# Decoding the sink group by two sequences at a time in a streaming-encoder step

## The chip, the cores and the metric

The kernel runs on one core of a Trainium2 chip. The metric is device time in microseconds (us) for one whole step, median over several executions. TensorE (PE) does the matmuls, VectorE (DVE), ScalarE (ACT) and GpSimd (POOL) the rest, and SyncE's queue (SP) issues nearly all transfers between HBM and SBUF. Each engine takes its instructions strictly in the order in which they were laid down for it, and semaphores make an engine wait for another's result.

## The reference

One layer of a hybrid encoder, on 512 prompt tokens and 8 decode sequences of 16 new tokens each (640 columns in all). One input projection is split between two groups of attention heads, whose outputs are normalised, joined and projected; a SwiGLU block and a final RMSNorm follow.

```python
def sample_layer(x, ck_a, cv_a, ck_b, cv_b, ...):          # 8 sequences of 16 new tokens
    qa, ka, va, qb, kb, vb = split_proj(rmsnorm(x, norm_mix) @ w_in)
    qb, kb = rope_partial(qb, pos), rope_partial(kb, pos)
    ...
    # group B: 16 query heads on 2 key/value heads, 128 cached keys + 16 new ones, learned sinks
    ob = band_attend(qb.reshape(b, 1, s, N_KV_B, GQA_R, HEAD_DIM),
                     concat([ck_b, kb], axis=1)[:, None], concat([cv_b, vb], axis=1)[:, None],
                     ones((1, keep_b + s)), sink=sinks.reshape(N_KV_B, GQA_R))
    return merge_and_ffn(x, oa, ob, ...), ka, va, kb, vb

def band_attend(q, k, v, valid, bias=None, sink=None):
    s = einsum('bgqhrd,bgkhd->bghrqk', q, k) * HEAD_DIM ** -0.5
    m = maximum(max(s, -1), sink);  p = exp(s - m)
    w = p / (sum(p, -1) + exp(sink - m))
    return einsum('bghrqk,bgkhd->bgqhrd', w, v)
```

For group B a decode sequence is therefore small: for each of the two key/value heads, 128 rows (8 query heads by 16 tokens) against 144 keys.

## The kernel before

Nearly all of the time is dense matmul work on PE: a weight tile is split into a high and a low part (`split`, L226 on ACT, L227 on DVE), and each product is three fp32r matmuls (`mm3`, L235 to L237) of 128x128 weights on 320 columns. I call these the **main** matmuls. The input projection does its first columns in plain form (`dense`, `proj`); the rest of it, and later the whole SwiGLU block, goes through `quartet`, a Strassen-like scheme with seven products on combined operands. Those combined operands of the input are made by `combine(k0, k1)` (L866 on DVE, L867 and L869 on POOL, then splits), for input tiles 0 to 2, 3 to 5 and 6 to 7.

Everything else, the attention above all, is written as Python generators that are drawn in between the main matmuls. `tick()` is called after each group of six main matmuls and, at a given `rate`, calls `pump()`; a pump runs one generator up to its next `yield`. I call that a **visit**. The streams (`heads`, `decode`, `combine`, later `norm`) take turns. A generator that yields `"part"` says that its next visit uses only a part of the PE array (64 rows or 64 columns), and the pump tries to run two such visits in a row. `get` hands out SBUF slots from fixed lists (S slots and twelve W slots) and itself pumps when a list is empty. A scheduler then settles the order of each engine.

`decode_b` is the decode attention of group B. It handles the 8 sequences one by one, in two halves of four. For one sequence it needs four visits: the scores (L596, two matmuls of 64 rows, one for each key/value head, each in a PSUM bank of its own) with the softmax on DVE and ACT (L601 to L611); two visits that only let time pass; four transposes of the weights (L341, through `tr`) and their copy out of PSUM on ACT (L621); the values (L626, on 64 columns) with the copy into the output tile `o_s` (L629). With the loads this makes 37 visits. `o_s` lies in a W slot; at the end it is stored to `ob_d` (L632), the slot goes back to the list, and `combine(6, 8)` is put into its queue:

```python
        dma(out=ob_d[:, :, SP:].rearrange("t p c -> p t c"), in_=o_s)
        n.put("W", os_b)
        n.put("S", kb, vb)
        n.add("combine", combine(6, 8))
```

The visits of `decode_b` are drawn in beside the last prompt heads of group B (`prompt_b`: scores L425, transposes L341 in `flip`, values L464) and beside four plain projections that end the first part of the input projection. After these, `n.drain()` runs what is left, and the quartets begin. About 240 us later comes the stage of the output projection of group B (`w_out_b`), into which the `heads` of group A (`prompt_a`), its decode (`decode_a`: L662, L671 to L678, L713) and the norm of group B (`norm_b`) are drawn in the same manner.

Of the kernel before, what the change touches and what calls it, by code (L numbers as in the profile page):

```python
# [7 lines left out]
AF = mybir.ActivationFunctionType  # L8
# [5 lines left out]
P = 128  # L14
# [4 lines left out]
SP = 512  # L19
# [3 lines left out]
DS = 16  # L23
CA = 256
CB = 128
# [294 lines left out]
def build(nc, tc, io, pools):  # L320
    n = Net(nc, tc, io, pools)
    dma = nc.sync.dma_start
# [12 lines left out]
    sinks, sink_d = col(16), col(2)  # L335
# [19 lines left out]
    qkv_d, sb_d = dram("qkv_d", (3, 8, P, TOK)), dram("sb_d", (P, 8, P))  # L355
# [13 lines left out]
    for kt in range(KT):  # L369
# [10 lines left out]
        own, hl = pair("S")  # L380
# [194 lines left out]
    def decode_b():  # L575
        os_b = n.get("W")
        o_s = sh(os_b, 8, P)
        for hf in range(2):
            ko, vo, qo, qraw = (n.get("S") for _ in range(4))
            k, v, q = sh(ko, 4, CB + DS), sh(vo, 4, P), sh(qo, 4, P)  # L580
            dma(out=k[:, :, :CB], in_=io["ckb"][:, 4 * hf:4 * hf + 4])
            dma(out=v, in_=io["cvb"][:, 4 * hf:4 * hf + 4])
            dma(out=sh(qraw, 8, 64), in_=sb_d[:, :, 64 * hf:64 * hf + 64])
# [3 lines left out]
            nc.gpsimd.tensor_copy(sh(qo, 4, 8, DS), sh(qraw, 8, 64).rearrange("p t (b s) -> p b t s", b=4))  # L587
            n.put("S", qraw)
            yield "part"
            for bb in range(4):  # L590
                b = 4 * hf + bb
                pss, pts = [], []
                for j in range(2):
                    rows = slice(64 * j, 64 * j + 64)
                    ps = n.bank()[:, :CB + DS]
                    nc.tensor.matmul(ps, q[rows, bb], k[rows, bb], start=True, stop=True)  # L596
                    pss.append(ps)
                for j, ps in enumerate(pss):
                    mx, den, se = n.small(1), n.small(1), n.small(1)
                    sk = sink_d[:, j:j + 1]  # L600
                    nc.vector.tensor_reduce(mx, ps, AX, ALU.max)  # L601
# [5 lines left out]
                    nc.scalar.activation(se, mx, AF.Exp, bias=sk)  # L607
                    nc.vector.tensor_tensor(den, den, se, ALU.add)
                    nc.vector.reciprocal(den, den)
                    nc.vector.tensor_scalar(pt[:, :CB], ex[:, :CB], den, None, ALU.mult)  # L610
                    nc.vector.tensor_scalar(pt[:, CB + DS * b:CB + DS * b + DS], ex[:, CB:], den, None, ALU.mult)  # L611
                    pts.append((t, pt))
                yield
                yield
# [6 lines left out]
                nc.scalar.activation(pt2[:, :4 * P], ps, AF.Identity)  # L621
                yield "part"
                po = n.bank()[:, :P]
                for x, vv in enumerate((v[:, bb], vb[:, SP:])):
                    for j in range(2):
                        nc.tensor.matmul(po[64 * j:64 * j + 64], vv[:, 64 * j:64 * j + 64],  # L626
                                         pt2[:, P * (2 * x + j):P * (2 * x + j) + P], start=x == 0, stop=x == 1)
# [4 lines left out]
        dma(out=ob_d[:, :, SP:].rearrange("t p c -> p t c"), in_=o_s)  # L632
        n.put("W", os_b)
        n.put("S", kb, vb)
        n.add("combine", combine(6, 8))
# [212 lines left out]
        n.put("S", x)  # L848

    sums = [[None] * 7 for _ in range(8)]  # L850
    thirds = []

    def combine(k0, k1):

# [2 lines left out]
        for kt in range(k0, k1):  # L857
# [9 lines left out]
            tt(s2, s1, a11, ALU.subtract)  # L867
            s3 = third[:, HT * (kt % 3):HT * (kt % 3) + HT]
            tt(s3, a21, a11, ALU.subtract)  # L869
            thirds.append((third, s3))  # L870
# [265 lines left out]
    parts = []  # L1136
# [293 lines left out]
```

## Time and profile before

| what | value |
|---|---|
| runs | 2541.51, 2544.72, 2547.5 us; median 2544.72 us |
| profiled execution | 2540.53 us, with a span of 2538.8 us from first to last instruction |
| PE busy | 2488.2 us, 98% of the span |
| DVE, ACT, POOL busy | 1966.8 us (77%), 1057.6 us (42%), 703.2 us (28%) |
| scores of group B's decode (L596) | from 210.7 to 268.1 us of the span |
| mean granted TensorE clock | 0.995 |

The numbers of the profile come from that one profiled execution, which took 4.2 us less than the median of the three runs. A line of the profile such as `L596` is a line of the kernel; `out<-in` names the tiles; `[0.66 <-DVE S L611]` behind a row says that the engine sat idle for 0.66 us until DVE's line 611 was done with an S tile.

### The profile page before, as it was taken

Reading aid. Unit: us, or ns where it says so; the run is one execution under the profiler, and the core shown is the slowest. Engines: PE = TensorE matmul, PEld = TensorE weight load, DVE = VectorE, ACT = ScalarE, POOL = GpSimd, SP = SyncE. Lnnn points to the kernel's source line nnn. Section 1 sums busy time; section 2 is a strip of 40 time slices with the busy share of each in tenths; the row PEclk is TensorE's granted clock in tenths of the full one; section 3 lists DMA queues with packets and bytes.
Section 4 is the critical chain, followed back from the end, with each engine's and each line's share of the span. In section 5 each row is a group of like instructions: output and inputs, shape, how many; then the busy total and the mean of one; then the engine's idle time right before and its main releaser. Section 6 shows DMA issues by size and latency. Waiting matters only on the chain.

```text
span 2538.8 us, 44665 instructions
## 1 busy us (share of the span) xinstructions
PE 2488.2 (98%) x17325; PEld 2422.5 (95%) x17325; DVE 1966.8 (77%) x2930; ACT 1057.6 (42%) x1701; POOL 703.2 (28%) x566
## 2 busy tenths in 40 slices
PE   8999999989999999999999999999999999999997
PEld 8898899988899999999999999999999999999997
DVE  6666767685567787788888888888889877777797
ACT  5445333355555544344343334334334333333343
POOL 0001211110021133323332332323335433333453
PEclk9999999999999999999999999999999999999998
DMA  6234433467863434444344334334437765666655
GB/s 197 83 98 131 148 123 127 135 235 244 263 219 139 140 130 138 149 156 134 128 130 146 120 127 144 133 128 131 145 120 247 249 170 165 182 171 172 186 160 183
DMA packets 191604, 401.68 MB, mean 158 GB/s; under 512 B 22496, under 2 KB 83936, under 8 KB 191392
## 3 DMA queue, kind: packets, MB, share of 16 engines
q1 hardware_dynamic: 167056, 344.75, 41.5%
q0 software_dynamic: 23184, 52.77, 7.6%
q8 instruction: 136, 2.23, 0.4%
q10 hardware_dynamic: 1152, 1.31, 0.2%
q14 instruction: 76, 0.62, 0.1%
HBM read 311.14 MB, written 86.87 MB: 157 GB/s over the span
## 4 chain that ended last, share of the span: by engine, by line
PE 87%; DVE 7%; DMA 2%; issue 1%; ACT 1%; POOL 0%; SPq 0%; DVEq 0%; ACTq 0%; POOLq 0%
PE dn L235 18%; PE dn L237 17%; PE dn L236 17%; PE at L235 10%; PE at L236 10%; PE at L237 10%; DVE W L227 2%; PE at L341 2%; PE at L464 1%; DMA W<-w_in 1%; PE at L425 1%; DVE S L793 1%; DMA W<-xT 1%; PE at L713 0%; ACT W L226 0%
## 5 line engine op out<-in xcount | busy, mean ns | idle before, releaser
L226 ACT ACTIVATE W<-W 128x1024 fp32r<-128x1024 f32 (+2 forms) x662 | 640.0, 968 | 1050.5 <-PE dn L236 554.9
L235 PE MATMUL dn<-S,W 128*128 128x320 f32 x3374 | 1055.9, 313 | 10.3 <-ACT W L226 5.1
L237 PE MATMUL dn<-S,W 128*128 128x320 f32 x3374 | 1046.3, 310 | 7.9 <-DVE W L227 7.7
L236 PE MATMUL dn<-S,W 128*128 128x320 f32 x3374 | 1044.7, 310 | 0.3 <-DVE S L227 0.3
L227 DVE TENSOR_TENSOR W<-W,W 128x1024 fp32r<-128x1024 f32 (+2 forms) x662 | 798.0, 1206 | 89.7 <-ACT W L226 85.5
L235 PEld LDWEIGHTS dn<-S,W 128*128 128x128 f32 x3374 | 635.0, 188 | 27.1 <-issue 13.8
L237 PEld LDWEIGHTS dn<-S,W 128*128 128x128 f32 x3374 | 634.4, 188 | 13.4 <-DVE W L227 11.7
L236 PEld LDWEIGHTS dn<-S,W 128*128 128x128 f32 x3374 | 635.1, 188 | 1.1 <-DVE S L227 0.6
L237 PE MATMUL at<-S,W 128*128 128x320 f32 x1834 | 567.4, 309 | 1.2 <-DVE W L227 1.0
L235 PE MATMUL at<-S,W 128*128 128x320 f32 x1834 | 567.6, 309 | 0.9 <-ACT W L226 0.9
L236 PE MATMUL at<-S,W 128*128 128x320 f32 x1834 | 567.0, 309 | 0.0
L774 POOL TENSOR_TENSOR W<-W,W 128x1024 f32<-128x1024 f32 (+2 forms) x84 | 181.3, 2158 | 771.9 <-DVE W L227 617.7
L237 PEld LDWEIGHTS at<-S,W 128*128 128x128 f32 x1834 | 344.5, 188 | 2.2 <-DVE W L227 1.9
L235 PEld LDWEIGHTS at<-S,W 128*128 128x128 f32 x1834 | 344.7, 188 | 1.4 <-ACT W L226 1.4
L236 PEld LDWEIGHTS at<-S,W 128*128 128x128 f32 x1834 | 344.7, 188 | 0.0
L793 DVE TENSOR_TENSOR S<-S,dn 128x320 f32<-128x320 f32 x398 | 182.2, 480 | 76.2 <-PE dn L237 75.7
L783 POOL TENSOR_TENSOR W<-W,W 128x1024 f32<-128x1024 f32 (+2 forms) x84 | 186.5, 2220 | 182.7 <-DVE W L227 136.4
L793 DVE TENSOR_TENSOR S<-S,at 128x320 f32<-128x320 f32 x292 | 138.3, 482 | 96.4 <-PE at L237 94.8
L767 DVE TENSOR_TENSOR W<-W,W 128x1024 f32<-128x1024 f32 (+2 forms) x86 | 119.9, 1394 | 37.7 <-DMA W<-w_gate 26.1
L771 DVE TENSOR_TENSOR W<-W,W 128x1024 f32<-128x1024 f32 (+2 forms) x86 | 97.9, 1139 | 59.1 <-DMA W<-w_up 29.4
L1082 POOL DMA_DIRECT2D S<-act_d x161 | 88.0, 547 | 166.7 <-PE dn L237 80.1
L1146 DVE TENSOR_TENSOR S<-S,half 128x320 fp32r<-128x320 f32 x147 | 119.8, 835 | 1.9
(157 smaller groups left out, 1703.2 us busy)
## 6 DMA issues: line engine op xcount, KB each, us to landing
S<-act_d POOLq DMA_DIRECT2D x161, 320.0 KB, 3.9
W<-w_gate SPq DMA_DIRECT2D x88, 512.0 KB
W<-w_up SPq DMA_DIRECT2D x88, 512.0 KB
W<-w_in SPq DMA_DIRECT2D x66, 512.0 KB
W<-w_down SPq DMA_DIRECT2D x64, 384.0 KB
act_d<-half SPq DMA_DIRECT2D x147, 160.0 KB
act_d<-S SPq DMA_DIRECT2D x147, 160.0 KB
W<-w_down SPq DMA_DIRECT2D x68, 320.0 KB
```

The costliest lines, as they stand in the source:

```text
L226: self.nc.scalar.activation(hi, src, AF.Identity)
L227: self.nc.vector.tensor_tensor(lo, src, f(hi), ALU.subtract)
L235: mm(out, a[0], b[0], start=first, stop=False)
L236: mm(out, a[0], b[1], start=False, stop=False)
L237: mm(out, a[1], b[0], start=False, stop=last)
L767: nc.vector.tensor_tensor(b12[:, w], b12[:, w], b22[:, w], sub)
L771: nc.vector.tensor_tensor(s6[:, w], b11[:, w], b12[:, w], sub)
L774: eng.tensor_tensor(b11[:, w], b22[:, w], s6[:, w], sub)
L783: eng.tensor_tensor(b21[:, w], b21[:, w], s6[:, w], sub)
L793: add = lambda o, a, b: nc.vector.tensor_tensor(o, a, b, ALU.add)
L1082: nc.gpsimd.dma_start(out=r(sh(t, 2, HT)), in_=r(act_d[which, :, j]))
L1146: nc.vector.tensor_tensor(r(src), src, hi, ALU.subtract)
```

## The change

`decode_b` handles two sequences in one step, so four steps instead of eight. The scores of both sequences go side by side into the same two banks (columns 0 and 256), eight transposes into two banks come in one visit, the values of both go into one bank, and the scores of the next step are issued in the same visit as the values. Four visits lie between the scores and the transposes instead of two, and two more between transposes and values; both halves are loaded near the start. With the loads this makes 31 visits, and 5 marks `"part"` instead of 16. Since `combine(6, 8)` can now be queued at another point than before, `thirds` becomes a table by tile number instead of a list.

```diff
+        def score(step):
+            (_, k, _, q), two = parts[step // 2], (2 * step % 4, 2 * step % 4 + 1)
+            pss = [n.bank() for _ in range(2)]
+            for i, bb in enumerate(two):
+                for j, ps in enumerate(pss):
+                    rows = slice(64 * j, 64 * j + 64)
+                    nc.tensor.matmul(ps[:, 256 * i:256 * i + CB + DS], q[rows, bb], k[rows, bb],
+                                     start=True, stop=True)
+            out = []
+            for i in range(2):
+                b, pts = 2 * step + i, []
                 for j in range(2):
-                    rows = slice(64 * j, 64 * j + 64)
-                    ps = n.bank()[:, :CB + DS]
-                    nc.tensor.matmul(ps, q[rows, bb], k[rows, bb], start=True, stop=True)
-                    pss.append(ps)
-                for j, ps in enumerate(pss):
+                    ps, sk = pss[j][:, 256 * i:256 * i + CB + DS], sink_d[:, j:j + 1]
                     mx, den, se = n.small(1), n.small(1), n.small(1)
-                    sk = sink_d[:, j:j + 1]
                     nc.vector.tensor_reduce(mx, ps, AX, ALU.max)
                     ...
+        parts = [load(0)]
+        yield
+        turn(parts[0][0], parts[0][3])
+        yield "part"
+        weights = score(0)
+        for step in range(4):
+            if step == 0:
+                parts.append(load(1))
+            for _ in range(4):
                 yield
-                yield
+            if step == 0:
+                turn(parts[1][0], parts[1][3])
+            turned = []
+            for pts in weights:
                 ps = n.bank()
                 for i, (_, pt) in enumerate(pts):
                     for x in range(2):
                         tr(ps[:, P * (2 * x + i):P * (2 * x + i) + P], pt[:, P * x:P * x + P])
                 n.put("S", *(t for t, _ in pts))
-                pt2 = n.get("S")
-                nc.scalar.activation(pt2[:, :4 * P], ps, AF.Identity)
-                yield "part"
-                po = n.bank()[:, :P]
-                for x, vv in enumerate((v[:, bb], vb[:, SP:])):
+                turned.append(n.get("S"))
+                nc.scalar.activation(turned[-1][:, :4 * P], ps, AF.Identity)
+            yield
+            yield
+            yield "part"
+            own, _, v, _ = parts[step // 2]
+            po = n.bank()
+            for i, pt2 in enumerate(turned):
+                for x, vv in enumerate((v[:, (2 * step + i) % 4], vb[:, SP:])):
                     for j in range(2):
-                        nc.tensor.matmul(po[64 * j:64 * j + 64], vv[:, 64 * j:64 * j + 64],
+                        nc.tensor.matmul(po[64 * j:64 * j + 64, P * i:P * i + P], vv[:, 64 * j:64 * j + 64],
                                          pt2[:, P * (2 * x + j):P * (2 * x + j) + P], start=x == 0, stop=x == 1)
-                n.put("S", pt2)
-                nc.vector.tensor_copy(o_s[:, :, DS * b:DS * b + DS], po.rearrange("p (t s) -> p t s", t=8))
-                yield "part" if bb < 3 else None
-            n.put("S", ko, vo, qo)
+            n.put("S", *turned)
+            if step < 3:
+                weights = score(step + 1)
+            for i in range(2):
+                at = DS * (2 * step + i)
+                nc.vector.tensor_copy(o_s[:, :, at:at + DS],
+                                      po[:, P * i:P * i + P].rearrange("p (t s) -> p t s", t=8))
+            if step % 2:
+                n.put("S", *own)
```

Lines after the change are numbered up to 30 higher: scores L599, softmax L607 to L617, copy of the transposes L642, values L651, copy to `o_s` L658, the store L662; `combine`'s loads of the input are L889 and L890 (L859 and L860 before), a quartet's loads L783 (L753).

**PE, a step of the decode.** Before, a values visit and the next score visit of one sequence (`dn` is the running projection, `at` a small bank):

```order
L235 MATMUL dn_2680<-S_61_197,W_489_2830 128x320
L626 MATMUL at_2854<-S_492_2846,S_462_2705 64x128 x2
L626 MATMUL at_2854<-S_492_2846,S_5_83 64x128 x2
L596 MATMUL at_2866<-S_461_2704,S_463_2706 128x144
L596 MATMUL at_2868<-S_461_2704,S_463_2706 128x144
L236 MATMUL dn_2680<-S_62_198,W_489_2830 128x320
```

After, the first step, from its second four transposes to the scores of the second step:

```order
L341 MATMUL at_2377<-cst,S_369_2237 128x128 x2
L341 MATMUL at_2377<-cst,S_373_2250 128x128 x2
L235 MATMUL dn_2439<-S_25_125,W_412_2441 128x320
L236 MATMUL dn_2439<-S_26_126,W_412_2441 128x320
L651 MATMUL at_2464<-S_399_2375,S_346_2138 64x128 x2
L651 MATMUL at_2464<-S_399_2375,S_5_83 64x128 x2
L651 MATMUL at_2464<-S_401_2382,S_346_2138 64x128 x2
L651 MATMUL at_2464<-S_401_2382,S_5_83 64x128 x2
L599 MATMUL at_2473<-S_345_2137,S_347_2139 128x144
L599 MATMUL at_2474<-S_345_2137,S_347_2139 128x144
L599 MATMUL at_2473<-S_345_2137,S_347_2139 128x144
L599 MATMUL at_2474<-S_345_2137,S_347_2139 128x144
```

Twice as much stands in one place, half as often; two main matmuls stand between the transposes and the values that read their copies.

**SP, the end of the decode.** Before: loads of the first quartets, then the store of `o_s` (W_344), then the load of the last operand of `combine` (tile 7), which has been given the W slot of `o_s`, then more loads of the quartets:

```order
L753 DMA W_582_3430<-w_in 128x1024
L753 DMA W_557_3186<-w_in 128x1024
L753 DMA W_583_3432<-w_in 128x1024
L632 DMA ob_d<-W_344_2136 128x8x128
L846 DMA o_va<-S_552_3176 128x640
L847 DMA qkv_d<-S_552_3176 128x640
L860 DMA W_545_3099<-xT 128x640
L753 DMA W_568_3298<-w_in 128x1024
```

After:

```order
L783 DMA W_543_3170<-w_in 128x1024
L889 DMA W_527_3021<-xT 128x640
L662 DMA ob_d<-W_344_2136 128x8x128
L783 DMA W_545_3174<-w_in 128x1024
L890 DMA W_528_3022<-xT 128x640
L876 DMA o_va<-S_532_3051 128x640
L877 DMA qkv_d<-S_532_3051 128x640
L783 DMA W_544_3172<-w_in 128x1024
```

The store and the last load of `combine` now stand ahead of most of the first quartet's weights. On PE the last values visit moved from row 1588, just ahead of the quartets (row 1601), to row 1473, 130 rows ahead of them (row 1603).

**ACT, the start of the `w_out_b` stage.** The visits there are drawn from the same turn-taking counter and the same slots, so that their order changes too, up to PE row 4215. Before, the first split for the third product of this stage (W_954) stands behind a block of table loads (`ACT_TABLE_LOAD`, 21 rows ahead), exponentials and copies:

```order
L573 ACTIVATE S_921_5849<-at_5850 128x512
L573 ACTIVATE S_923_5862<-at_5863 128x512
L673 ACTIVATE S_930_5890,sm_5887<-S_929_5889,sm_5886 128x256
L674 ACTIVATE S_930_5890,sm_5888<-S_929_5889,sm_5886 128x16
L454 ACTIVATE S_946_5946<-at_5941 128x512
L454 ACTIVATE S_948_5959<-at_5954 128x512
L226 ACTIVATE W_955_5975<-W_954_5974 128x1024
```

After, it stands ahead of the table loads (W_942):

```order
L438 ACTIVATE S_837_5512,sm_5698<-S_837_5512,sm_5697 128x512
L573 ACTIVATE W_856_5578<-at_5722 128x512
L226 ACTIVATE W_943_5963<-W_942_5962 128x1024
L276 ACT_TABLE_LOAD
L276 ACTIVATE sm_5756<-sm_5754 128x6
L438 ACT_TABLE_LOAD
L438 ACTIVATE S_831_5506,sm_5764<-S_831_5506,sm_5763 128x128
```

The split moved by 24 rows on ACT, while the matmuls that read it moved by 4 rows on PE (3412 before, 3408 after).

More of the change, by code (lines that the diff above doesn't have):

```diff
@@ L577, in decode_b, with load @@
         o_s = sh(os_b, 8, P)
-        for hf in range(2):
-            ko, vo, qo, qraw = (n.get("S") for _ in range(4))
-            k, v, q = sh(ko, 4, CB + DS), sh(vo, 4, P), sh(qo, 4, P)
+        def load(hf):
+            own = [n.get("S") for _ in range(4)]
+            k, v, q = sh(own[0], 4, CB + DS), sh(own[1], 4, P), sh(own[2], 4, P)
             dma(out=k[:, :, :CB], in_=io["ckb"][:, 4 * hf:4 * hf + 4])
             dma(out=v, in_=io["cvb"][:, 4 * hf:4 * hf + 4])
-            dma(out=sh(qraw, 8, 64), in_=sb_d[:, :, 64 * hf:64 * hf + 64])
+            dma(out=sh(own[3], 8, 64), in_=sb_d[:, :, 64 * hf:64 * hf + 64])
@@ L584, in decode_b @@
             nc.gpsimd.tensor_copy(k[:, :, CB:],
                                   kb[:, SP + 64 * hf:SP + 64 * hf + 64].rearrange("p (b s) -> p b s", b=4))
-            yield
-            nc.gpsimd.tensor_copy(sh(qo, 4, 8, DS), sh(qraw, 8, 64).rearrange("p t (b s) -> p b t s", b=4))
-            n.put("S", qraw)
-            yield "part"
-            for bb in range(4):
-                b = 4 * hf + bb
-                pss, pts = [], []
-                for j in range(2):
-                    rows = slice(64 * j, 64 * j + 64)
-                    ps = n.bank()[:, :CB + DS]
-                    nc.tensor.matmul(ps, q[rows, bb], k[rows, bb], start=True, stop=True)
-                    pss.append(ps)
-                for j, ps in enumerate(pss):
+            return own, k, v, q
@@ new lines, in turn @@
+        def turn(own, q):
+            nc.gpsimd.tensor_copy(sh(own[2], 4, 8, DS), sh(own[3], 8, 64).rearrange("p t (b s) -> p b t s", b=4))
+            n.put("S", own.pop())
+        def score(step):
[9 more added lines that the diff above has]
+                b, pts = 2 * step + i, []
+                for j in range(2):
+                    ps, sk = pss[j][:, 256 * i:256 * i + CB + DS], sink_d[:, j:j + 1]
@@ L612, in decode_b @@
                     pts.append((t, pt))
+                out.append(pts)
+            return out
+        parts = [load(0)]
[7 more added lines that the diff above has]
+            for _ in range(4):
                 yield
-                yield
+            if step == 0:
+                turn(parts[1][0], parts[1][3])
+            turned = []
+            for pts in weights:
                 ps = n.bank()
@@ L869, in combine @@
             tt(s3, a21, a11, ALU.subtract)
-            thirds.append((third, s3))
+            thirds[kt] = third, s3
             for which, x in ((3, s1), (1, s2), (6, a12)):
```

3 lines of the change are left out of this document (1 added, 2 removed).

## The prediction

> **What bounds the kernel now.** I read the page first: PE's share and the chain that ended last.
>
> ```profile
> PE 2488.2 (98%) x17325; PEld 2422.5 (95%) x17325; DVE 1966.8 (77%) x2930; ACT 1057.6 (42%) x1701; POOL 703.2 (28%) x566
> PE 87%; DVE 7%; DMA 2%; issue 1%; ACT 1%; POOL 0%; SPq 0%; DVEq 0%; ACTq 0%; POOLq 0%
> ```
>
> PE is the bound, so that a change off PE counts only where PE waits. How much there is to win is read by stage: columns are PE busy, its weight loads, DVE, ACT, POOL, then granted clock, DMA share, GB/s.
>
> ```profile
> 205.00:280.00 75.00, 71.89 (x506) 62.26 (x505) 51.46 (x175) 40.16 (x112) 15.22 (x23) 1.00 0.42 135
> 280.00:320.00 40.00, 36.62 (x241) 35.01 (x240) 28.36 (x30) 12.55 (x15) 7.53 (x4) 1.00 0.44 150
> 320.00:500.00 180.00, 178.40 (x1210) 177.17 (x1210) 122.22 (x129) 55.81 (x58) 35.75 (x15) 1.00 0.37 129
> 500.00:560.00 60.00, 56.87 (x371) 53.03 (x370) 48.04 (x101) 30.52 (x50) 11.45 (x14) 0.97 0.74 246
> 560.00:580.00 20.00, 16.12 (x135) 14.13 (x138) 9.86 (x26) 14.64 (x38) 1.48 (x5) 0.91 0.48 165
> 580.00:760.00 180.00, 178.94 (x1594) 150.97 (x1583) 112.26 (x336) 95.02 (x244) 21.95 (x41) 1.00 0.73 243
> ```
>
> The undisturbed quartets (third row) lose 1.6 us in 180, and one main matmul takes 180/1210 = 0.149 us there. PE is idle for 3.1 us beside the decode (75 - 71.89) and 3.4 us in the first quartets behind it; the `w_out_b` stage, which the change reorders too, loses 3.1, 3.9 and 1.1 us in its three stretches, and in the middle one the clock is down. The waits of the first two stretches (total, times, longest):
>
> ```profile
> PE at L341 <- DVE S L610: 1.8, 4, 1.0
> PE at L341 <- DVE S L611: 1.3, 4, 0.7
> PE dn L237 <- DVE W L227: 1.2, 2, 1.0
> PE dn L235 <- ACT W L226: 1.1, 1, 1.1
> PE dn L235 <- ACT S L226: 0.6, 1, 0.6
> PE at L235 <- ACT W L226: 0.4, 1, 0.4
> ```
>
> 3.1 us are transposes that wait for the decode's softmax; the rest are splits that the quartets wait for.
>
> **A. Fewer visits on PE.** A visit costs more than its matmuls, because PE changes between full and partial use of the array. A values visit, a score visit, and both in a row:
>
> ```profile
> 242.93 0.31 PE L237 MATMUL dn<-S,W 128*128 128x320 f32 x1
> 243.17 0.66 PE L626 MATMUL at<-S,S 128*64 128x128 f32 x8
> 244.01 0.31 PE L236 MATMUL dn<-S,W 128*128 128x320 f32 x1
> ...
> 236.62 0.31 PE L237 MATMUL dn<-S,W 128*128 128x320 f32 x1
> 236.86 0.52 PE L596 MATMUL at<-S,S 64*128 64x144 f32 x4
> 237.56 0.31 PE L236 MATMUL dn<-S,W 128*128 128x320 f32 x1
> ...
> 253.78 0.31 PE L235 MATMUL dn<-S,W 128*128 128x320 f32 x1
> 254.05 0.66 PE L626 MATMUL at<-S,S 128*64 128x128 f32 x8
> 254.64 0.52 PE L596 MATMUL at<-S,S 64*128 64x144 f32 x4
> 255.09 0.42 PE L236 MATMUL dn<-S,W 128*128 128x320 f32 x1
> 255.34 0.31 PE L237 MATMUL dn<-S,W 128*128 128x320 f32 x1
> ```
>
> In each piece I take the time from the main matmul before the visit to the second one after it, less two main steps (0.30): 1.08 - 0.30 = 0.78 us for values, 0.94 - 0.30 = 0.64 for scores, 1.56 - 0.30 = 1.26 for both in a row. Before, there are eight of each, and in the order four pairs stand in a row: 8 x 0.78 + 8 x 0.64 - 4 x 0.16 = 10.7 us. After, there are four of each with twice the matmuls, three pairs in a row. The added matmuls cost at most 0.59 (254.64 - 254.05) for values and 0.45 (255.09 - 254.64) for scores, which gives 3 x 2.30 + 1.37 + 1.09 = 9.4 us. If they step by their columns as the main ones do (0.149 x 128/320 = 0.06 and 0.149 x 144/320 = 0.067), they cost 0.48 and 0.27, and the sum is 8.2. So A is -1.3 to -2.5 us; I take -1.8, since in the third step the order tears the values in two, which gives back about one change of use (0.3).
>
> **B. The transposes' waits.** They do not simply go: four softmax chains instead of two run through DVE one behind the other. From a score visit on:
>
> ```profile
> 228.97 0.52 PE L596 MATMUL at<-S,S 64*128 64x144 f32 x4
> 229.62 0.30 DVE L601 TENSOR_REDUCE sm<-at 128x1 f32<-128x144 f32 x1
> 231.12 0.16 DVE L608 TENSOR_TENSOR sm<-sm,sm 128x1 f32<-128x1 f32 x1 [0.73 <-ACT sm L607]
> 231.71 0.23 DVE L611 TENSOR_SCALAR S<-S,sm 128x16 f32<-128x16 f32 x1
> 232.12 0.16 DVE L608 TENSOR_TENSOR sm<-sm,sm 128x1 f32<-128x1 f32 x1 [0.18 <-ACT sm L607]
> 259.78 0.60 ACT L621 ACTIVATE S<-at 128x512 f32<-128x512 f32 x1
> ```
>
> The first head's weights are done 3.0 us after the scores begin (231.94), each further chain takes 1.0 (231.12 to 232.12): 4.0 us for one sequence, 6.0 for two, more where DVE's order puts other work between. Against that stands what PE has to do in between, counted in the new order with 0.149 for a main row. Step 1: 12 main rows (1.8), the scores (0.9) and eight prompt score matmuls at two main steps each (2.4), then four transposes: the second four come some 5.7 us after the scores, and the last chain has four prompt reductions between its rows, so they wait about 1 us; then only two main rows cover the two copies of 0.60 each, about 0.5 more. Step 2: over 40 rows, no wait. Step 3: the first transposes come 2.5 us after the scores (eight prompt values and three main rows), and the last ones have two longer DVE rows in their chain: about 1.7 in all. Step 4: 36 main rows, but two splits and three `combine` operations on DVE ahead: about 1. Sum 4.2 against 3.1: B is +1.1 us. Ends: -3.1 (all waits covered) and +4 (twice my estimate). The loads of the second half and their copies on POOL move to step 1 and hide, as POOL is busy for 15 of 75 us.
>
> At one place a rule speaks against the change. The Trainium skill (PSUM — Partial Sum Buffer, PSUM bank collisions) says that TensorE writing and another engine reading the same bank and quadrant at once is an error, and that software keeps them apart by bank. Two sequences now share a bank, so by it the first reduction would wait for all scores of the step. In the trace the first reduction starts 0.65 us after the scores begin (229.62 - 228.97); by that rule it would be later by the added scores, 0.27 to 0.45 us, four times, B would be up to 1.8 higher, and the whole sum -3.9 instead of -5.7. No run so far shows it.
>
> **C. The first quartets.** The last operand of `combine` (tile 7) uses the W slot of `o_s`:
>
> ```profile
> 279.07 0.38 SPq L632 DMA_DIRECT2D ob_d<-W  x1
> 283.21 0.33 SPq L860 DMA_DIRECT2D W<-xT  x1
> 286.21 0.55 DVE L866 SCALAR_TENSOR_TENSOR W<-W,gains,W 128x320 f32<-128x320 f32 x1
> 286.84 0.88 POOL L867 TENSOR_TENSOR W<-W 128x320 f32<-128x320 f32 x1 [7.67 <-DVE W L866]
> 288.28 0.42 PE L235 MATMUL dn<-S,W 128*128 128x320 f32 x1 [0.57 <-ACT S L226]
> ```
>
> The store goes out at 279.07, the load 4.1 us later, the operand reaches PE at 288.28, and the products around it stand torn and wait again. With the last values 130 PE rows ahead of the quartets instead of 13, this chain of some 9 us ends inside 130 x 0.149 = 19 us of main work. The three ACT waits go (0.6 + 1.1 + 0.4) and with each the slow first step behind it (0.42 for 0.31): -2.3 us. Ends: 0 (another split late instead) and -3.3 (the two DVE waits as well). SP is blocked for those 4.1 us ahead of the quartet's own loads; the 19 us cover that.
>
> **D. The `w_out_b` stage.** Its work is the same, in another order. Here one wait can be followed:
>
> ```profile
> 568.46 1.06 ACT L226 ACTIVATE W<-W 128x1024 fp32r<-128x1024 f32 x1
> 569.58 0.41 PE L235 MATMUL dn<-S,W 128*128 128x320 f32 x1 [2.50 <-ACT W L226]
> 571.51 0.42 PE L237 MATMUL dn<-S,W 128*128 128x320 f32 x1 [1.38 <-DVE W L227]
> 570.00:575.00 5.00, 3.62 (x18) 3.46 (x18) 2.92 (x8) 2.99 (x8) 0.85 (x1) 0.70 0.61 214
> ```
>
> The split that PE waits for starts on ACT at 568.46, behind the block of exponentials and copies; in the new order it stands 24 rows earlier on ACT, while its matmuls move by 4 rows. The two waits (2.50 + 1.38 = 3.9 us) then have no ground. The half clock behind them (0.70 in 570 to 575, so 0.30 x 5 = 1.5 us) may go with them; I take half, 0.8. The Trainium skill (TensorE: Matmul & The Clock Gate, Part 1) says that the clock is halved after an idle window of about 3.4 us and freed after a busy one; by that rule the whole 1.5 us would go, and the sum would be -6.4. The trace agrees so far as the low clock does follow the stretch in which PE idles. Against this: an order that is only shuffled makes waits of its own. The three stretches idle for 8.1 us now (3.1 + 3.9 + 1.1); I put a quarter of that, 2.0, as new waits. D is -3.9 - 0.8 + 2.0 = -2.7 us. Ends: -5.4 (no new waits, whole clock window back) and +4 (the waits stay, half of 8.1 added).
>
> **Sum.** -1.8 + 1.1 - 2.3 - 2.7 = -5.7 us. Against the profiled execution of 2540.53 us that is 2534.8; the median of the runs stands 4.2 us higher, so against it 2544.72 - 5.7 = 2539.0. The other stages keep their order on every engine. Adding all good ends gives -14.3, all bad ones +6.7. About 0.2% (5 us) is what a measurement of this kernel can tell from no change, and the sum lies close to it.
>
> **Rivals.**
> - *Given back, within 0.2% (2544).* A holds, but B reaches its upper end or D's new waits eat the gain: -1.8 + 3 - 1.5 + 0 = about 0, between 2540 and 2549. For it: the DVE chain of 6 us is longer than the PE work in three of four steps, and nothing fixes the order of the `w_out_b` stage. Against it: C and D's waits each have a cause that can be followed to a row which has moved.
> - *Slower (2551).* The place is the decode step. Since values and next scores share a visit, a late transpose now holds up both the values and the scores that feed the next four chains, and main rows behind it on PE's in-order queue wait too. It decides from the point where the fourth chain ends more than 3 us after PE gets to its transposes: 4 steps x 3 = 12 us, against 3.1 now, makes B +9, and without D's gain the sum is -1.8 + 9 - 1 = about +6. For it: DVE is busy 51 of 75 us there, and in the third step PE reaches the transposes 2.5 us after the scores. Against it: the longest such wait now is 1.0 us, with the same order of margins.
> - *Bank sharing* by the rule above is a form of the first rival: about 2541.
>
> **Chances.** The forecast, faster by more than 0.2%: 0.56, with a range of its own from 2530 to 2539.6. Given back: 0.37. Slower by more than 0.2%: 0.07. The sum lies a little past the edge, and the larger side of its spread (whole clock window, no new waits) lies beyond it; so the time I name is 2538.5, the rounded sum. The range goes from 2529 (a gain of 16: all good ends, and a little of the 3 us by which single runs stand off their median) to 2547, halfway into what is left of the second case above no change; that leaves about 1 in 10 on either side.
>
> **What would show it.** A: PE's time around a values visit of 16 and scores of 8 passes at or under 2.3 us. B: the waits of the transposes for DVE (L616, L617) between 3 and 6 us in total, and a short wait of the first values for ACT's copies; two reductions that start only after the last score of a step would speak for the bank rule. C: the store to `ob_d` some 17 us or more ahead of the first quartet, no main matmul there that waits for a split of an S tile. D: the waits of 2.5 and 1.4 us gone at the third product of `w_out_b`, and no half clock behind it. It would be wrong if the `w_out_b` stage showed new waits above 4 us, if PE waited more than 3 us in one decode step, or if the clock fell in another place.

## The result, and the profile after

The changed kernel takes 2529.98 us in the median against 2543.68 for the kernel before on the same chip: a ratio of 0.9947, with a 95% interval of 0.9935 to 0.9959, or 13.7 us less. The forecast was 2538.5 with a range of 2529 to 2547: the sign was right and the time lies at the fast end of the range, with a gain more than twice the forecast sum of 5.7. (The time named, 2538.5, lies half a microsecond under what that sum gives against the first median, 2539.0.) The profiled execution after took 2528.33 us with a span of 2526.6, which is 12.2 less than the span before.

First the stretches of the span, in the columns of before (PE, its weight loads, DVE, ACT, POOL, granted clock, DMA share, GB/s).

```profile
205.00:280.00 75.00, 73.58 (x528) 66.57 (x527) 55.10 (x181) 40.87 (x115) 16.48 (x25) 0.98 0.50 158
280.00:320.00 40.00, 37.34 (x249) 36.32 (x249) 26.46 (x28) 11.99 (x13) 7.23 (x3) 1.00 0.33 116
320.00:500.00 180.00, 179.28 (x1217) 178.12 (x1216) 122.54 (x130) 55.64 (x58) 33.82 (x14) 1.00 0.38 132
500.00:560.00 60.00, 57.11 (x398) 52.76 (x397) 49.30 (x107) 35.80 (x68) 11.02 (x15) 1.00 0.73 246
560.00:580.00 20.00, 20.00 (x197) 16.55 (x196) 10.44 (x36) 12.69 (x33) 1.73 (x8) 1.00 0.86 290
580.00:760.00 180.00, 178.66 (x1547) 151.26 (x1546) 111.64 (x325) 93.00 (x236) 20.50 (x36) 1.00 0.70 231
```

The decode's stretch idles for 1.4 us instead of 3.1, but its clock is no longer whole (0.98). The fifth row is the largest change: PE is busy for all 20 us at full clock, where it was idle for 3.9 us at 0.91. What PE still waits for from 205 to 320 us, and in the `w_out_b` stage (500 to 760):

```profile
PE dn L237 <- DVE W L227: 1.6, 3, 0.5
PE dn L235 <- DVE S L410: 1.1, 1, 1.1
PE at L425 <- ACT S L612: 0.9, 1, 0.9
PE at L341 <- DVE S L616: 0.5, 2, 0.3
```

```profile
PE at L425 <- DVE sm L428: 2.1, 3, 1.2
PE dn L237 <- DVE W L227: 1.7, 2, 1.2
PE at L341 <- DVE sm L428: 0.4, 1, 0.4
```

The transposes (L341) wait for 0.5 us in place of 3.1, and the three ACT waits of the first quartets are gone, as are the 2.5 and 1.4 of the `w_out_b` stage. Two waits are new: prompt scores (L425) until a decode exponential (L612, the third of that step's four, which ends at 216.46 us) is done with its bank, and the first quartet for a projection's copy out of PSUM (L410).

To see where the 12.2 us lie, I set the start of the k-th main matmul after against that before: the difference is -0.4 us at the 1000th, -4.9 at the 1575th (first quartets done), -5.9 at the 3000th, -7.9 at the 3100th, -14.2 at the 3150th, and from the 3700th on it stays at -12.7 to -12.9. So it comes from two places, decode with first quartets (-4.5) and `w_out_b` (-6.8); -1.0 lies in the quartets between.

### The profile page after: what moved, and what is told of

Its sections match the earlier page's. It is cut to its first block, busy times and chain, and to the rows that moved or that the text cites. A ratio compares the mean times of both kernels' runs of the same rounds, so it can differ in the third digit from the quotient of the medians.

```text
span 2526.6 us, 44669 instructions
## 1 busy us (share of the span) xinstructions
PE 2484.5 (98%) x17325; PEld 2420.7 (96%) x17325; DVE 1965.5 (78%) x2930; ACT 1055.0 (42%) x1701; POOL 701.9 (28%) x566
## 4 chain that ended last, share of the span: by engine, by line
PE 88%; DVE 7%; issue 2%; DMA 2%; ACT 1%; SPq 0%; POOL 0%; DVEq 0%; ACTq 0%; POOLq 0%
PE dn L235 18%; PE dn L237 18%; PE dn L236 17%; PE at L235 10%; PE at L237 10%; PE at L236 10%; DVE W L227 2%; PE at L341 2%; PE at L464 1%; PE at L425 1%; DVE S L823 1%; DMA W<-w_in 1%; PE at L743 0%; DMA W<-xT 0%; ACT S L438 0%
## 5 line engine op out<-in xcount | busy, mean ns | idle before, releaser
L227 DVE TENSOR_TENSOR W<-W,W 128x1024 fp32r<-128x1024 f32 (+2 forms) x662 | 800.3, 1209 | 90.5 <-ACT W L226 83.2
L797 DVE TENSOR_TENSOR W<-W,W 128x1024 f32<-128x1024 f32 (+2 forms) x86 | 117.4, 1365 | 40.8 <-DMA W<-w_gate 29.4
```

Of the source, the lines that this page charges most:

```text
L227: self.nc.vector.tensor_tensor(lo, src, f(hi), ALU.subtract)
L797: nc.vector.tensor_tensor(b12[:, w], b12[:, w], b22[:, w], sub)
```

## What the trace says about the half clock

The record of the granted clock shows half clock in whole stretches of 3.41 us, on a grid of that length which stands differently to the program in each execution. Before, there are two in the `w_out_b` stage (from 548.1 and 572.0 us); after, none there, but one in the decode, from 219.1 on:

```profile
215.00:220.00 5.00, 4.10 (x19) 2.91 (x19) 4.86 (x32) 1.96 (x9) 0.00 (x0) 0.91 0.24 84
220.00:225.00 5.00, 5.00 (x40) 4.35 (x39) 2.45 (x11) 3.77 (x13) 0.61 (x3) 0.75 0.28 77
```

The place is the first step: the new bank wait of 0.9 us stands there among partial matmuls with few columns. This is one of the signs that I had named for being wrong, a clock that falls in another place.

```profile
215.40 0.31 PE L236 MATMUL dn<-S,W 128*128 128x320 f32 x1
216.61 1.13 PE L425 MATMUL at<-S,S 64*128 64x256 f32 x4 [0.90 <-ACT S L612]
...
219.07 1.97 PE L341 MATMUL at<-cst,S 128*128 128x128 f32 x8
```

A stretch at half clock costs up to 3.41 x 0.5 = 1.7 us, and this upper end is what I take for each. Since it is drawn anew in each execution, I count it apart below. For each kernel I take PE's **excess**: the time between successive main matmuls beyond 0.1467 us each, summed over main matmuls 1000 to 1575 (decode and first quartets) and 3000 to 3700 (`w_out_b`), from the starts in the trace, and beside it the number of half-clock stretches there.

## The experiments

Where an experiment should leave the `w_out_b` stage as it is, the counter of turns is set to a fixed number at its start.

**The w_out_b order alone, without the new decode (e1), and the new decode without that order (e2).** The counter that deals out the visits is the only thing that carries the change into the stage: with it shifted by two, the stage of each kernel has, row by row on PE and ACT, the order of the other.

```diff
             n.streams = (("heads 0", "heads"), ("decode 0", "decode"), ("heads 1", "heads"), ("decode 1", "decode"))
+            n.turn += -2        # e1, in the kernel before;  e2, in the changed kernel: += 2
```

> The kernel before, with the decode untouched; only the counter of turns is lowered by 2 where the streams for the w_out_b stage are set, which gives that stage the order of visits on PE and ACT that it has after the change. Theory (the w_out_b part of the gain, 6.4 us in the step between its 3100th and 3150th main matmul, is nothing but a newly drawn order): 6 to 7 us under the kernel before, about 2537; the waits of 2.5 and 1.4 us at the third product and both half-clock stretches at 548 and 572 us are gone. Rival (the gain there comes from the new decode itself: its stores, slots or memory traffic): within 1 us of the kernel before, waits and half clock as before.

> The changed kernel, with the counter raised by 2 at the same place, so that the w_out_b stage has the order of before. Theory (order alone): 6 to 7 us above the changed kernel, about 2536.5, which leaves 6 to 7 us of gain for the decode and the first quartets; the waits of 2.5 and 1.4 us are back, and half clock with them. Rival (the decode itself): stays at 2530, without those waits.

e1: 2535.87 us, ratio to before 0.9972 [0.9961, 0.9983], -7.1 us. e2: 2536.93, ratio 0.9979 [0.9970, 0.9988], -5.3. Together -12.4 of the 13.7. In e1 (first fence, a stretch of the span) the middle of the stage is whole and the two waits are gone, though one half-clock stretch falls earlier in the stage (from 550.8 us), which my theory had excluded; in e2 (second and third, waits from 500 to 760 us and the same stretch) they are back, with half clock:

```profile
560.00:580.00 20.00, 20.00 (x210) 18.34 (x209) 11.59 (x41) 17.52 (x53) 1.38 (x6) 1.00 0.56 172
```

```profile
PE dn L237 <- DVE W L227: 2.6, 2, 1.4
PE dn L235 <- ACT W L226: 2.5, 1, 2.5
...
```

```profile
560.00:580.00 20.00, 16.13 (x155) 14.80 (x154) 8.81 (x30) 11.91 (x31) 1.60 (x5) 0.91 0.66 219
```

So about half of the measured gain has nothing to do with how the decode works: it is a counter that stood at another number. The rival fell in both.

**The third order (e3).** As I work it out from the program, the counter modulo eight gives three orders in all; this is the one that neither kernel has.

```diff
+            n.turn = 323        # in the changed kernel, at the same place
```

> The changed kernel with the counter set so that the w_out_b stage gets the third and last order that the counter can give. In it the split for the third product also stands ahead of ACT's table loads. Theory (that one split decides): within 2 us of the changed kernel, 2528 to 2532, no wait of 2 us or more for ACT there. Rival (the whole order is a draw, and the changed kernel drew a lucky one): 3 to 7 us above it, in other waits.

2533.66 us, ratio 0.9968 [0.9955, 0.9980], 3.7 us above the changed kernel by the medians, and 5.3 by the ratios. The waits of 2.5 and 1.4 us stay away, but another one comes, further on in the stage, with half clock behind it (from 706.9 us):

```profile
706.34 0.66 PE L341 MATMUL at<-cst,S 128*128 128x128 f32 x4 [3.00 <-ACT S L454]
```

My theory that one split decides fell, the rival held: each order has waits of its own, and the changed kernel drew the best of three.

**Is the decode's part a draw too (e5, e6)?** The old decode in the two other orders that a shift at its own streams gives.

```diff
     n.streams = (("heads 0", "heads"), ("decode 0", "decode"), ("combine", "combine"))
+    n.turn += 1             # e5;  e6: += 2;  both in the kernel before
```

> The kernel before, its decode by single sequences, but with the counter of turns raised by 1 where the decode's streams are set: the visits of heads, decode and combine are drawn in another order up to the first quartets, and the w_out_b stage is held to its order of before. Theory (the 5 to 6 us that the changed decode gains with the w_out_b order of before come from fewer and larger visits): within 2 us of the kernel before, 2541 to 2545; excess of PE's time over its main steps from main matmul 1000 to 1575 between 29 and 33 us, against 31.6 before and 27.1 after. Rival (that part of the gain is a lucky draw too): 2539 or less, excess under 29 us.

> The same with the counter raised by 2, the third and last draw of the decode before. Theory: 2541 to 2545, excess 29 to 33 us. Rival: 2539 or less, excess under 29 us.

2542.80 us, ratio 1.0002 [0.9994, 1.0011], and 2543.80, ratio 1.0001 [0.9992, 1.0010]. The excess is 32.2 and 34.6 us, that of e6 a little above what I expected. All three draws of the old decode take the same time, so the gain does not come from an unlucky draw of the old one.

**The new decode in another draw (e7).** The same shift by 1 in the changed kernel.

> The changed kernel with the counter raised by 1 where the decode's streams are set, the w_out_b stage held to its order of after. Fifteen main rows instead of eleven then stand between the first prompt scores and the next ones, so that their wait for a bank shrinks from 0.9 to about 0.3 us. Theory (the gain belongs to the visits, not to the draw): within 2 us of the changed kernel, 2528 to 2532, excess 25 to 29 us. Rival (a draw): 2533 or more, excess over 29 us.

2531.95 us, ratio 0.9962 [0.9950, 0.9975]: the time is at the theory's edge, the excess (30.7) above it, where the rival stood, because two half-clock stretches (from 214.3 and 251.8 us) fell into it; without their 3.4 us it is 27.3. The bank wait did vanish, but scores wait for a copy on POOL:

```profile
PE at L599 <- POOL S L590: 2.0, 1, 2.0
PE dn L235 <- DVE S L410: 1.5, 1, 1.5
PE at L341 <- DVE S L616: 1.3, 1, 1.3
...
```

That copy (L590) itself waits for a load from `sb_d`. It is no mark of this draw: the changed kernel has the same wait in its second profile (e11), where the copy starts at 212.82 us instead of 211.68:

```profile
PE at L599 <- POOL S L590: 1.4, 1, 1.4
```

Beside e1, the old decode with the same later order (0.9972), the ratio leaves only 0.0010, some 2.5 us, for the new decode in this draw, where e2 gives 5.3. The intervals overlap and the third draw of the new decode was not run, so how much of its gain hangs on the draw stays open.

**Fewer visits between scores and transposes (e4, e9).** Four `yield`s in a row are three visits that only let time pass (before the change, two `yield`s and one such visit); I go on counting the `yield`s.

```diff
-            for _ in range(4):
+            for _ in range(2):        # e4;  e9: range(3)
                 yield
```

> The changed kernel with two visits instead of four between the scores and the transposes, and the w_out_b stage held to its order. Theory (the four visits are what covers the four softmax chains of 6 us): the transposes' waits for DVE rise from 0.5 to 2 to 4 us; on the other side the prompt scores stand 49 rows behind the first decode scores, so that their wait of 0.9 us for a bank and the half clock at 219 us (1.6 us) go: in sum -0.5 to +1.5 us against the changed kernel. Rival (main rows between the pieces cover the chains in any case): waits stay under 1 us, and it is 2 to 3 us faster than the changed kernel.

> The changed kernel with three visits instead of four between scores and transposes, the w_out_b stage held to its order of after. As with two visits, the prompt scores then stand 48 rows behind the first decode scores instead of 11. Theory (what the changed decode gives back is the bank wait of 0.9 us and the half-clock stretches behind it; each stretch of 3.4 us costs 1.7): no wait for L612, no half clock between 205 and 260 us, waits of the transposes under 1.5 us, excess of PE over its main steps from main matmul 1000 to 1575 of 25 to 26.5 us, and 1 to 2 us under the changed kernel in the median. Rival (the room that is won is lost to the transposes, as with two visits): excess of 27 us or more, same time as the changed kernel.

e4: 2529.91 us, ratio 0.9952 [0.9938, 0.9966]; e9: 2528.61, ratio 0.9946 [0.9933, 0.9958], beside 2528.59 and 0.9942 for the changed kernel itself. As expected the bank wait and the half clock beside the decode are gone, in both. But the room goes elsewhere; the waits from 200 to 330 us in e4, then in e9:

```profile
PE dn L237 <- DVE W L227: 3.6, 3, 2.5
PE at L341 <- DVE S L617: 0.9, 2, 0.7
PE at L341 <- DVE S L616: 0.6, 1, 0.6
...
```

```profile
PE at L341 <- DVE S L617: 2.5, 4, 1.2
PE at L341 <- DVE S L616: 1.0, 1, 1.0
...
```

With three visits the transposes wait for 3.5 us, not under 1.5; with two they wait for 1.5, less than my 2 to 4, and a quartet waits for a split. With four it was 0.5 (0.7 in e11). The wait does not simply grow as the visits get fewer, since another number of visits also deals out the whole order anew; but four cover the softmax chains best here, and what is won by fewer is spent. In e4 the theory's time held; in e9 the excess (26.2) lies in the theory's range, while the time is the rival's. No version here beats the changed kernel.

**The next scores in a visit of their own (e10).**

```diff
             for i in range(2):
                 at = DS * (2 * step + i)
                 ...
+            if step < 3:
+                yield "part"
+                weights = score(step + 1)
```

(with the two lines that stood ahead of the loop taken out).

> The changed kernel with the next scores in a visit of their own behind the values, w_out_b held to its order of after. Theory (joining values and scores saves 0.16 us a pair, so that pairs and the room for the softmax chains both matter little): within 1.5 us of the changed kernel. Rival (the joint visit is what brings the decode's gain): 3 us or more slower than it.

2533.69 us, ratio 0.9963 [0.9951, 0.9976], 5.1 us above the changed kernel beside it: the rival held. The excess is 31.4 us with two half-clock stretches, 28.0 without. The transposes wait again, since the scores come later than the values while the transposes don't:

```profile
PE dn L237 <- DVE W L227: 2.3, 2, 2.0
PE at L341 <- DVE S L616: 2.2, 2, 1.8
PE at L341 <- DVE S L617: 1.0, 2, 0.6
...
```

So the joint visit seems worth more than the 0.16 us a pair that it saves on PE: it starts the softmax one visit earlier. How much of the 5.1 us is half clock by chance, one profile doesn't tell; without the stretches the excess is 2.2 above the 25.8 of the changed kernel. The three added visits also deal out the order anew, and e7 shows that another draw alone can cost some of this.

**The slot of the decode's output alone (e8).** In the kernel before, `o_s` keeps its W slot until the projections have ended, so that tile 7 of `combine` is loaded into another.

```diff
-        n.put("W", os_b)
+        held.append(os_b)
...
     n.drain()
+    n.put("W", *held)
```

> The kernel before, where only the W slot of the decode's output is handed back after the decode and the projections have ended, so that tile 7 of combine gets another slot and its load does not wait for the store. The w_out_b stage is held to its order of before. Theory (step C: the late operand tears the first products): the three ACT waits of 0.4 to 1.1 us in the first quartets go, and it is 1.3 to 2.5 us faster than before, 2540 to 2541.5. Rival (the quartets wait for DVE's and ACT's splits in any case): other waits of the same size, within 1 us of before.

2541.51 us, ratio 0.9994 [0.9985, 1.0003]. The three ACT waits are gone, and what is left from 275 to 330 us is:

```profile
PE dn L237 <- DVE W L227: 1.0, 2, 0.5
PE at L341 <- DVE S L612: 0.4, 1, 0.4
PE at L237 <- DVE W L227: 0.4, 1, 0.4
```

Gaps between two main matmuls with nothing in between fall from 7.15 to 4.50 us in main matmuls 1000 to 1575, so the mechanism of C is shown, with a size of 2.65 us in this trace; the time alone can't be told from no change.

**The changed kernel once more (e11).**

> The changed kernel itself, unchanged, beside the two others on the same chip. Theory (half-clock stretches of 3.4 us, on a grid of that length that stands at random to the program, make the spread of single runs): the same order on every engine, and yet the decode's half-clock stretch at 219 us may be missing or moved, and the w_out_b stage may have one; 2528 to 2532 in the median. Rival (the stretches belong to the program): half clock at 219 us again, and nowhere else before 1900 us.

2528.59 us, ratio 0.9942 [0.9929, 0.9956]. This execution has full clock at 220 us and a half-clock stretch from 544.0 on, where the first profile had none:

```profile
220.00:225.00 5.00, 5.00 (x46) 3.99 (x45) 4.03 (x21) 2.85 (x10) 0.62 (x3) 1.00 0.14 23
540.00:545.00 5.00, 3.31 (x16) 2.32 (x15) 4.94 (x22) 0.00 (x0) 0.10 (x1) 0.90 0.95 306
545.00:550.00 5.00, 5.00 (x32) 4.99 (x30) 3.62 (x16) 3.01 (x10) 0.21 (x1) 0.76 0.99 340
```

Every engine has the same order as in the first profile, and the stretches lie in other places: the rival is out. (The theory, which said only that they may move, could hardly have failed.)

All profiles side by side (excess in us, and half-clock stretches of 3.4 us in that part):

| kernel | decode, first quartets | w_out_b | order of w_out_b |
|---|---|---|---|
| before | 31.6, 0 | 107.8, 2 | of before |
| e5, e6 | 32.2, 0; 34.6, 0 | 107.5, 2; 106.9, 1 | of before |
| e8 | 29.9, 0 | 110.4, 4 | of before |
| e1 (old decode) | 33.7, 0 | 102.5, 1 | of after |
| e2 (new decode) | 27.7, 1 | 106.7, 1 | of before |
| e3 | 28.6, 2 | 104.7, 1 | the third |
| after, e11 | 27.1, 1; 26.7, 0 | 101.0, 0; 102.6, 1 | of after |
| e4, e9 | 27.2, 0; 26.2, 0 | 101.0, 0; 101.0, 0 | of after |
| e7, e10 | 30.7, 2; 31.4, 2 | 101.2, 0; 101.0, 0 | of after |

Without 1.7 us a stretch, the old decode in its own draw stands at 32.7 (before, e1) and the new one at 25.8 (mean of after, e2, e3, e11): -6.9 us. The four executions of the new one have four stretches, the two of the old one none: +1.7 on average, which makes -5.2 beside e2's -5.3. The stage without stretches stands at 104.4 in the order of before (five profiles) and 101.0 in that of after (seven): -3.4; the stretches are 2.0 an execution against 0.3: -2.9. That is -6.3, beside e1's -7.1. The other draw of the new decode (e7) is left out here; without stretches it stands at 27.3.

## Why the prediction was right, and where it was not

By its terms the profiled pair gained 2.7 us in A, nothing in B, 1.8 in C, 6.8 in D and 1.0 in the quartets between, 12.3 in all, where I had 1.8, -1.1, 2.3 and 2.7. The direction is earned by A, C and the two waits of D. That more than half of the gain comes from D, whose order is a draw, is luck, and only the wide fast end of the range holds it.

- **A, fewer visits: right, a little too small.** Excess in visits without the waits and the stretch at half clock: before 24.6 - 3.1 = 21.5, after 21.9 - 1.4 - 1.7 = 18.8, so -2.7 us; I had -1.8 (ends -1.3 and -2.5). The other profile of each order gives 21.9 (e1) and 19.5 (e11), so -2.4. The joint visit came out a little cheaper than priced: sixteen value passes and eight scores take 237.09 - 235.37 = 1.72 us (first fence), where eight and four took 255.09 - 254.05 = 1.04, so 0.68 more (I had 0.75 to 1.04). The sign that I had named, 2.3 us or less for the whole visit, can be read in e11, where the first one runs at full clock (second fence): 224.07 - 221.75 - 0.30 = 2.02 us.

```profile
235.37 1.09 PE L651 MATMUL at<-S,S 128*64 128x128 f32 x16
236.40 0.76 PE L599 MATMUL at<-S,S 64*128 64x144 f32 x8
237.09 1.74 PE L464 MATMUL at<-S,S 128*64 128x256 f32 x16
```

```profile
221.75 0.30 PE L236 MATMUL dn<-S,W 128*128 128x320 f32 x1
222.06 1.14 PE L651 MATMUL at<-S,S 128*64 128x128 f32 x16
223.13 0.76 PE L599 MATMUL at<-S,S 64*128 64x144 f32 x8
223.82 0.42 PE L237 MATMUL dn<-S,W 128*128 128x320 f32 x1
224.07 0.31 PE L235 MATMUL dn<-S,W 128*128 128x320 f32 x1
```

  The decode's scores or values break into the main work at 6 places instead of 11. Transposes by themselves do so no less often (13 places instead of 12), so they don't explain what I had too little.
- **B, the transposes' waits: wrong in sign.** Predicted 3 to 6 us, measured 0.5. The chains were no shorter than I said: from the start of the scores to the last weights 6.7 us in the first step (219.17 - 212.49) and 7.2 in the third, where I had 6 and more. What failed is the count of PE's work against them: PE gets to the transposes 6.6 us after the scores in the first step (219.07 - 212.49), where I had 5.1, and 3.0 in the third (239.37 - 236.40), where I had 2.5. In the third the late partial visits are longer than I took them (the sixteen L464 passes above last 1.66 us to the next start). In the first, 0.9 us is a wait that I had not listed: a bank is now held until the exponential of its second sequence, prompt scores wait for it, and half clock follows (1.7 when it falls so). Waits and clock together: -1.7 + 1.7 = 0 in the profiled pair, against +1.1 in the sum. In e11 the first scores also wait 1.4 us for POOL; that the second half's loads and copies hide, as I had it, is therefore not sure, but the old decode has such a wait too in e5 (1.0).
- **The bank rule: the program decides.** The prediction's 0.65 us is no clean base, since DVE was busy until then; where it was idle, the first reduction before starts 0.55 us after the scores (first two rows). After, only the third step shows a reduction that waits for scores, at 237.19 - 236.40 = 0.79 us (third row), so 0.24 later, near my 0.27. In the first step (0.88 us) DVE was busy with a split until then, and in the fourth the reduction starts at 243.89, while the last passes of the scores, in the other bank, start at 243.84 and 244.06. So it waits for its own bank's scores and not for all of the step, as I had put it. In the trace only the last score of a bank counts up the semaphore for which the reduction waits, so that the program itself brings the wait about; what the chip would do without it no run shows. The Trainium skill (PSUM — Partial Sum Buffer, PSUM bank collisions) has software keep the engines apart in this way, by bank, and the trace agrees as far as the program does so. PE did not wait for it in a place that shows.

```profile
210.72 0.52 PE L596 MATMUL at<-S,S 64*128 64x144 f32 x4
211.27 0.31 DVE L601 TENSOR_REDUCE sm<-at 128x1 f32<-128x144 f32 x1 [3.38 <-PE at L596]
...
237.19 0.31 DVE L607 TENSOR_REDUCE sm<-at 128x1 f32<-128x144 f32 x1 [0.19 <-PE at L599]
```

- **C, the first quartets: right in mechanism, near in size.** The store goes out at 258.78, 18 us ahead of the first quartet (about 277), and no main matmul waits for a split of an S tile. The gaps between main matmuls fall by 7.15 - 5.31 = 1.8 us (I had 2.3); e8 alone gives 2.65. The same measure stands at 7.6 in e1 (old decode) and at 4.4, 4.9 and 5.2 in e11, e2 and e3 (new decode; 1.7 taken off the last two for a stretch at half clock), so that over all of them it falls by some 2.5. What e8 has more than the first profile is about the size of a new wait, for L410: DVE has the projection's copy behind a weight sum (L797) that itself waits for a transfer.

```profile
258.78 0.38 SPq L662 DMA_DIRECT2D ob_d<-W  x1
...
278.63 2.01 DVE L797 TENSOR_TENSOR W<-W,W 128x1024 f32<-128x1024 f32 x1 [1.35 <-DMA W<-w_in]
280.56 0.81 DVE L410 TENSOR_TENSOR S<-dn,S 128x640 f32<-128x640 f32 x1
```

- **D, the w_out_b stage: right in sign and cause, far too small** (-2.7 against -6.8, beyond my end of -5.4). The two waits went as followed to their rows (-3.4, as the stage without stretches shows, of the -3.9). The term that failed is the +2.0 for new waits: there were none. That it could have been otherwise shows e3, whose order brought a 3.0 us wait and gains only 3.1 in the stage; so this is the luck of the draw. And the half clock went nearly whole: I had seen the one stretch that the row of 570 to 575 us shows and taken half of it, 0.8; there were two, and the runs put it at 2.9 on average. The Trainium skill (TensorE: Matmul & The Clock Gate, Part 1) says that the window of 3413 ns runs freely and does not start anew with the kernel; the stretches of 3.41 us that move between e11 and the first profile agree.
- **The quartets between** gave -1.0 (1.5 us of waits for L227 became 0.5), which I had at nothing. It need not be the change: from the 1575th to the 3000th main matmul the two profiles of the changed kernel take 212.4 and 213.9 us (e11), the kernel before 213.3, and the old decode in e1 211.9.
- The rivals: "given back" needed late transposes or new waits in the `w_out_b` stage, "slower" very late transposes, and neither came. The worry behind the slower one was sound: with the next scores set apart (e10) the transposes wait for 3.2 us.

## What to carry to other kernels

When a change alters how many turns a generator takes, and a counter deals out the turns of all that follows, measure the change twice: once with the counter set back, so that the later order is held. Here that separates some 5 us of decode, part of which may hang on a draw of its own, from some 7 us of luck, and the three orders to be had differ by as much as the change is worth. A forecast should then treat a redrawn stage as a draw between its known worst waits gone and others come, and not set a quarter of the idle time against it: here new waits were none in one order and 3.0 us in another.

## What the runs showed of the hardware

When half clock comes is sharper than I had expected, and not a matter of idle time alone. I counted, over the 13 profiles, the columns that PE's matmuls stream in each stretch of 3.41 us of the clock's grid (7360 in the median stretch, 9369 stretches at full clock from 30 to 2500 us). Of 29 stretches with fewer than 2600 columns, all 29 were followed by half clock; of 10 with 2600 to 3100, four; of 9330 with more, none. The two limits are drawn from these same profiles and were not tried on others. By this count a wait of 2.5 us costs up to 1.7 more when it falls into one stretch, and may cost nothing more when the grid cuts it in two; and densely packed partial matmuls with few columns, as in the first decode step, fall below the limit with only 0.9 us of waiting (2368 columns in the stretch from 215.6 us of the first profile). That is part of why executions of one kernel differ with every instruction in the same order: of the 2.3 us between the two profiles of the changed kernel, 1.6 lie in the `w_out_b` stage, where only one has a stretch at half clock. How much of the whole spread of 8.3 us (2526.66 to 2534.92) it makes, times without a profile don't show.
